# A reciprocal square root seeded by a power on GpSimd, with one Newton step

## The chip, the core and the metric

One core of a Trainium2 chip runs the whole program. The metric is the device time of one execution in microseconds (us); the median of three runs is given. The engines of the core work in parallel, each through its own queue in a fixed order, and wait for each other at semaphores: TensorE (PE) multiplies matrices, VectorE (DVE) and ScalarE (ACT) do elementwise work, GpSimd (POOL) issues small DMAs and fills buffers here, and SyncE (SP) issues the DMAs of the weights.

## What is computed

Two blocks of a diffusion transformer, one after the other, on 256 tokens of width 1024, in float32. Each block has two layers, each layer a mixing and a feed-forward part, and each part is modulated by vectors that come from a conditioning input. The norms between and inside the parts are where a reciprocal square root is taken:

```python
def layer_norm(x, g, b):
    mu = jnp.mean(x, axis=-1, keepdims=True)
    var = jnp.mean(jnp.square(x - mu), axis=-1, keepdims=True)
    return (x - mu) * lax.rsqrt(var + 1e-5) * g + b

def rms_norm(x, g):
    return x * lax.rsqrt(jnp.mean(jnp.square(x), axis=-1, keepdims=True) + 1e-6) * g

# first block
x = layer_norm(x, ln0_g, ln0_b)
for layer in range(2):
    y = hybrid_mixer(x * (1 + scale) + shift, ...)   # scan, latent attention, spatial gating
    x = layer_norm(DN_ALPHA * x + (1 + gate) * y, ...)
    y = swiglu(...) if layer == 0 else moe_swiglu(...)   # 8 experts, top 2
    x = layer_norm(DN_ALPHA * x + (1 + gate) * y, ...)
# second block
for l in range(2):
    h = rms_norm(x, norm_mix) * (1 + sc_a) + sh_a
    ...   # two kinds of attention, with rms_norm of q, k and of each head's output
    x = x + g_a * (concat([o_m, o_d]) @ w_out)
    h = rms_norm(x, norm_ffn) * (1 + sc_f) + sh_f
    x = x + g_f * ((silu(h @ w_gate) * (h @ w_up)) @ w_down)
```

## The kernel before

The program runs eight steps: 1 and 3 are the hybrid mixers, 2 a dense feed-forward part, 4 the experts, 5 and 7 attention, 6 and 8 feed-forward parts. The 256 tokens are two tiles of 128 rows, t = 0 and 1, with tokens on partitions; the products want the transposed rows, so between the steps rows are normalised, then transposed on PE (L175), then scaled and shifted (make_h, L501 to L506, or make_hf, L483).

Every weight block is split into an exact high and low part, high by a cast on ACT (L147), low by a subtraction on DVE (L148), and multiplied three times (L166 to L168). These splits are most of DVE's and ACT's work. The modulation vectors are sums over rows of a big matrix, made on DVE (L292, L294, tile macc) and closed by PE (L171), in portions that are filled in behind other work.

The reciprocal square root is one helper, rsqrt(v, n), for n numbers on each of 128 partitions. It takes half of v (L182), a first guess by integer arithmetic on v's bit pattern (L184), and three Newton steps, each two instructions for n = 1 (L188, L193) and three for more (L190, L191, L193): 8 or 11 DVE instructions, each needing the one before. It is called 38 times: 14 times with n = 1 (twice in layer_norm at the start; in resid at the boundaries 1 to 2, 2 to 3, 3 to 4, 5 to 6, 6 to 7, 7 to 8, once for each token tile), twice with n = 2 in resid_rms between steps 4 and 5, and 22 times in the mixers and the attentions, with n from 2 to 16. What takes its result at a boundary is L562 or L564 for t = 0 on DVE, and for t = 1 L557 and L558, or L560, of which L558 and L560 are on ACT (at 2 to 3 both tiles take L562). In step 3 the norm of the latent attention is taken by L865 and L866, in step 5 the norm of queries and keys by L1377.

A scheduler sets the order of each engine's queue when the program is built; work that is filled in (splits, modulation) is kept behind the last instruction of the last normalisation by the method behind. In step 4 the gate's modulation sum (eight blocks of rows, L294, closed by L171 on PE) is put in before make_hf and the router, and PE's queue holds its L171 ahead of the transposes for the router.

Of the kernel before, what the change touches and what calls it, by code (L numbers as in the profile page):

```python
# [20 lines left out]
KD = 8  # L21
# [38 lines left out]
# the second block's attention, in units of four heads: Q queries and keys, V values, A attention, F modulation  # L60
# [3 lines left out]
class _Net:  # L64
# [22 lines left out]
    def phase(self, **sizes):  # L87
        """Scratch pools of one part of the program."""
# [34 lines left out]
    def behind(self):  # L123
        """Vector work that is issued behind the last normalisation's short steps."""
# [14 lines left out]
    def split_now(self, v):  # L139
        """Exact high and low parts of a [128, k, n] block: two lists of k tiles."""  # L140
# [18 lines left out]
    def mm3(self, out, a, b, start, stop):  # L159
        """out += a^T b, a and b given as exact (high, low) parts."""  # L160
# [17 lines left out]
    def rsqrt(self, v, n):  # L178
        """1/sqrt of v (> 0) to float32 accuracy."""
        V = self.nc.vector  # L180
        vh = self.sc([128, n])
        V.tensor_scalar(vh, v, 0.5, None, ALU.mult)  # L182
        y = self.sc([128, n])
        V.tensor_scalar(y.bitcast(I32), v.bitcast(I32), -0.5, float(0x5F3759DF - 2 ** 31), ALU.mult, ALU.add)  # L184
        for _ in range(3):
            u = self.sc([128, n])
            if n == 1:
                V.scalar_tensor_tensor(u, y, vh[:, 0:1], y, ALU.mult, ALU.mult)  # L188
            else:
                V.tensor_tensor(u, y, y, ALU.mult)  # L190
                V.tensor_tensor(u, u, vh, ALU.mult)  # L191
            y2 = self.sc([128, n])
            self.last = V.scalar_tensor_tensor(y2, u, 1.5, y, ALU.subtract, ALU.mult)  # L193
            y = y2
        return y

    def evac_split(self, ps, hi, lo, A=None, B=None):
        """ps [128, 2, n] in PSUM -> exact parts of ps * A + B (columns per middle index)."""
# [30 lines left out]
    def fill(self, n):  # L229
        """n more blocks of two rows of 128 of the modulation's product, behind the rest."""  # L230
# [220 lines left out]
    def two_rows(self, g, b):  # L451
# [3 lines left out]
        return gb  # L455

    def affine(self, x, g, b):
        """x * g + b in place, with rows g and b from DRAM."""
        V = self.nc.vector
        gb = self.two_rows(g, b)  # L460
        for t in range(2):
# [1141 lines left out]
```

## Time and profile before

| what | value |
|---|---|
| median of three runs | 2099.36 us (2097.38 to 2099.42) |
| the profiled execution's own span | 2100.0 us |
| PE busy | 1959.5 us, 93% of the span |
| DVE busy | 1658.0 us, 79%, 2512 instructions |
| ACT busy | 1208.3 us, 58% |
| POOL busy | 50.1 us, 2%, 98 instructions |

The page gives for each engine its busy time and its share of the span. Its fourth part follows the work that ended last back to the start, and tells for each engine what share of the span lies on that chain. The table by stretches tells the busy time of each engine in a piece of the span; what PE lacks to the length of the piece is time in which it stood still. A timeline's row is the start, the duration, the engine, the line of the program, the operation, and what it writes and reads; in brackets stands how long the engine had been idle and what ended that.

### The profile page before, as it was taken

What the parts mean: (1) busy time and instruction counts of PE and PEld (TensorE: products, weight loads), DVE (VectorE), ACT (ScalarE), POOL (GpSimd) and SP (SyncE); (2) the same over time, 40 slices, a digit from 0 to 9 for tenths busy, and PEclk for the clock granted to TensorE, in tenths of its full rate; (3) what the DMA queues carried; (4) which work ended last, traced back from release to release, by engine and by line L of the source; (5) the groups of instructions that cost most, each with busy time, mean ns of one, the idle gap of its engine ahead of it and who ended that gap; (6) DMA issues with size and microseconds to landing.
All of it is one profiled execution on the core that took longest, in us unless ns stands there. A gap on an engine that the chain in (4) does not pass through costs nothing.

```text
span 2100.0 us, 30041 instructions
## 1 busy us (share of the span) xinstructions
PE 1959.5 (93%) x11481; PEld 1681.4 (80%) x11481; DVE 1658.0 (79%) x2512; ACT 1208.3 (58%) x1817; POOL 50.1 (2%) x98
## 2 busy tenths in 40 slices
PE   3998999898599999999999999969989999998999
PEld 3887999886478787878778887858869998978998
DVE  6888977897588888888888888889778877667554
ACT  3454444452378767767776777755454446545442
POOL 4000000100000000000000000000000000000000
PEclk9999999998599999999999999979999999999999
DMA  9585998565489999899989999958339894326662
GB/s 319 181 287 202 339 331 308 177 224 204 141 300 360 328 339 334 317 358 346 340 322 348 344 360 351 360 181 278 124 132 346 322 320 147 121 87 214 203 199 80
DMA packets 283238, 555.25 MB, mean 264 GB/s; under 512 B 10172, under 2 KB 137520, under 8 KB 283088
## 3 DMA queue, kind: packets, MB, share of 16 engines
q1 hardware_dynamic: 280000, 549.49, 74.6%
q0 software_dynamic: 2656, 3.20, 0.8%
q8 instruction: 91, 1.49, 0.3%
q10 hardware_dynamic: 432, 0.58, 0.1%
q14 instruction: 59, 0.48, 0.1%
HBM read 552.19 MB, written 1.05 MB: 263 GB/s over the span
## 4 chain that ended last, share of the span: by engine, by line
PE 64%; DVE 5%; ACT 2%; issue 1%; DMA 1%; ACTq 0%; DVEq 0%
PE pp L167 12%; PE pp L168 11%; PE pp L166 11%; PE pa L634 6%; PE ya L167 4%; PE ya L166 4%; PE ya L168 4%; PE pp L175 3%; PE pj L166 1%; PE pj L167 1%; PE pj L168 1%; PE pp L171 1%; DVE lo L148 1%; PE sa L171 1%; ACT hi L147 1%
## 5 line engine op out<-in xcount | busy, mean ns | idle before, releaser
L148 DVE TENSOR_TENSOR lo<-raw,hi 128x1024 fp32r<-128x1024 f32 x660 | 787.5, 1220 | 193.1 <-ACT hi L147 191.5
L147 ACT CAST hi<-raw 128x1024 fp32r<-128x1024 f32 x660 | 668.4, 1051 | 393.6 <-PE pp L167 157.9
L166 PE MATMUL pp<-h,hi 128*128 128x256 f32 x960 | 274.4, 286 | 0.0
L168 PE MATMUL pp<-h,lo 128*128 128x256 f32 x960 | 271.6, 283 | 0.0
L167 PE MATMUL pp<-h,hi 128*128 128x256 f32 x960 | 271.5, 283 | 0.0
L148 DVE TENSOR_TENSOR lo<-rawx,hi 128x1024 fp32r<-128x1024 f32 x176 | 208.5, 1220 | 42.4 <-ACT hi L147 42.3
L294 DVE SCALAR_TENSOR_TENSOR macc<-raw,const,macc 128x1024 f32<-128x1024 f32 x168 | 215.3, 1281 | 6.6 <-DMA raw<-in_ada_w_dram 2.3
L167 PEld LDWEIGHTS pp<-h,hi 128*128 128x128 f32 x960 | 184.1, 192 | 1.9 <-issue 1.2
L166 PEld LDWEIGHTS pp<-h,hi 128*128 128x128 f32 x960 | 184.0, 192 | 1.8 <-ACT hi L147 1.0
L168 PEld LDWEIGHTS pp<-h,lo 128*128 128x128 f32 x960 | 184.1, 192 | 0.0
L147 ACT CAST hi<-rawx 128x1024 fp32r<-128x1024 f32 x176 | 176.5, 1048 | 11.9 <-PE pp L168 9.9
L166 PE MATMUL pj<-hi,h 128*128 128x256 f32 x576 | 169.6, 295 | 8.2 <-ACT h L505 3.7
L167 PE MATMUL pp<-lo,h 128*128 128x512 f32 (+1 forms) x480 | 174.6, 364 | 1.2 <-DVE lo L148 1.0
L166 PE MATMUL pp<-hi,h 128*128 128x512 f32 (+1 forms) x480 | 173.0, 361 | 0.0
L167 PE MATMUL pj<-lo,h 128*128 128x256 f32 x576 | 166.0, 290 | 0.8 <-DVE lo L148 0.8
L168 PE MATMUL pj<-hi,h 128*128 128x256 f32 x576 | 165.9, 290 | 0.0
L634 PE MATMUL pa<-hi,s 128*128 128x512 f32 x528 | 151.5, 396 | 0.0
L167 PE MATMUL pp<-lo,xe 128*128 128x512 f32 (+1 forms) x384 | 146.5, 382 | 1.3 <-DVE lo L148 1.0
L166 PE MATMUL pp<-hi,xe 128*128 128x512 f32 (+1 forms) x384 | 145.2, 379 | 0.0
L168 PE MATMUL pp<-hi,xe 128*128 128x512 f32 (+1 forms) x384 | 144.7, 377 | 0.0
L168 PE MATMUL pp<-hi,x 128*128 128x512 f32 (+1 forms) x384 | 143.2, 373 | 0.0
L167 PE MATMUL ya<-lo,s 128*128 128x512 f32 x352 | 141.9, 403 | 0.0
(481 smaller groups left out, 3563.3 us busy)
## 6 DMA issues: line engine op xcount, KB each, us to landing
raw<-in_moe_w_dram SPq DMA_DIRECT2D x176, 1024.0 KB, 6.1
rawx<-in_moe_w_dram SPq DMA_DIRECT2D x88, 1024.0 KB, 6.5
raw<-in_ada_w_dram SPq DMA_DIRECT2D x48, 1024.0 KB, 6.9
raw<-in_w_mod_dram SPq DMA_DIRECT2D x48, 1024.0 KB, 6.3
raw<-in_w_in_dram SPq DMA_DIRECT2D x42, 1024.0 KB, 5.8
raw<-in_ffn_w_dram SPq DMA_DIRECT2D x33, 1024.0 KB, 6.1
raw<-in_w_gate_dram SPq DMA_DIRECT2D x22, 1024.0 KB, 5.4
raw<-in_w_up_dram SPq DMA_DIRECT2D x22, 1024.0 KB, 5.5
```

Of the source, the lines that this page charges most:

```text
L147: self.nc.scalar.copy(h, v[:, z:z + m])
L148: self.nc.vector.tensor_tensor(l, v[:, z:z + m], h.bitcast(F32), ALU.subtract)
L166: mm(out, lhsT=a[0], rhs=b[0], start=start, stop=False)
L167: mm(out, lhsT=a[0], rhs=b[1], start=False, stop=False)
L168: mm(out, lhsT=a[1], rhs=b[0], start=False, stop=stop)
L171: self.nc.tensor.matmul(out, lhsT=lhsT, rhs=rhs, start=start, stop=stop)
L175: self.nc.tensor.transpose(out, in_, self.ident[:p, :p])
L294: V.scalar_tensor_tensor(acc, v[:, i], c, acc, ALU.mult, ALU.add)
L634: mm(accs[t][h], lhsT=y[ia][:, s], rhs=W[ib][:, h * 512:(h + 1) * 512], start=start and ia == 0 and ib == 0, stop=stop and ia == 1)
```

## The change

rsqrt takes its first guess as the power v^(-1/2) on GpSimd, against a constant tile mhalf that holds -0.5 (a new memset on POOL at the start), and runs one Newton step in place of three. DVE then runs three instructions for n = 1 (L184, L187, L192 of the changed file) and four for more (L184, L189, L190, L192), and POOL one (L182). The sign of half of v is turned, so that the step adds 1.5 where it subtracted. Comments and docstrings that are left out as well move the line numbers: what was L292 and L294 is L290 and L292, what was L327 is L325.

```diff
     def rsqrt(self, v, n):
         V = self.nc.vector
+        y = self.sc([128, n])
+        self.nc.gpsimd.tensor_tensor(y, v, self.mhalf[:, 0:1].to_broadcast([128, n]) if n > 1 else self.mhalf, ALU.pow)
         vh = self.sc([128, n])
-        V.tensor_scalar(vh, v, 0.5, None, ALU.mult)
-        y = self.sc([128, n])
-        V.tensor_scalar(y.bitcast(I32), v.bitcast(I32), -0.5, float(0x5F3759DF - 2 ** 31), ALU.mult, ALU.add)
-        for _ in range(3):
-            u = self.sc([128, n])
-            if n == 1:
-                V.scalar_tensor_tensor(u, y, vh[:, 0:1], y, ALU.mult, ALU.mult)
-            else:
-                V.tensor_tensor(u, y, y, ALU.mult)
-                V.tensor_tensor(u, u, vh, ALU.mult)
-            y2 = self.sc([128, n])
-            self.last = V.scalar_tensor_tensor(y2, u, 1.5, y, ALU.subtract, ALU.mult)
-            y = y2
-        return y
+        V.tensor_scalar(vh, v, -0.5, None, ALU.mult)
+        u = self.sc([128, n])
+        if n == 1:
+            V.scalar_tensor_tensor(u, y, vh[:, 0:1], y, ALU.mult, ALU.mult)
+        else:
+            V.tensor_tensor(u, y, y, ALU.mult)
+            V.tensor_tensor(u, u, vh, ALU.mult)
+        y2 = self.sc([128, n])
+        self.last = V.scalar_tensor_tensor(y2, u, 1.5, y, ALU.add, ALU.mult)
+        return y2
...
+        self.mhalf = self.tl("const", [128, 1], tag="mhalf")
+        nc.gpsimd.memset(self.mhalf, -0.5)
```

The scheduler orders the queues anew. The first place is the start of the program. POOL's queue there, before, from the end of the small operands' DMAs (b_mod is the bias of the second block's modulation):

```order
L391 DMA sh_126<-in_diff_subln_dram 2x128
L370 DMA sh_144<-in_b_mod_dram 96x128
L425 DMA t_391<-in_ssd_dt_bias_dram 128x8
L425 DMA t_393<-in_ssd_a_log_dram 128x8
L425 DMA t_395<-in_ssd_d_dram 128x8
```

And after; ISA is an entry that loads code for POOL, and L182 are the powers of the two token tiles:

```order
L391 DMA sh_128<-in_diff_subln_dram 2x128
L370 DMA sh_146<-in_b_mod_dram 96x128
L182 ISA
L182 TENSOR_TENSOR t_161<-t_155,const_105 128x1
L182 TENSOR_TENSOR t_180<-t_174,const_105 128x1
L425 DMA t_377<-in_ssd_dt_bias_dram 128x8
```

Both powers now stand behind the DMA issues of the small operands. DVE's queue at the start, after (macc_190 is the first modulation sum, macc_218 the second, t_155 is v of the first tile, L325 takes the first sum from PE):

```order
L445 TENSOR_SCALAR t_155<-t_154 128x1
L290 TENSOR_SCALAR macc_190<-raw_191,const_113 128x1024
...
L292 SCALAR_TENSOR_TENSOR macc_190<-raw_203,const_113,macc_190 128x1024 x2
L187 SCALAR_TENSOR_TENSOR t_165<-t_161,t_163 128x1
L192 SCALAR_TENSOR_TENSOR t_167<-t_165,t_161 128x1
L325 SCALAR_TENSOR_TENSOR col_207<-pp_208,const_119 128x8
L447 TENSOR_TENSOR t_156<-t_153,t_167 128x1
L290 TENSOR_SCALAR macc_218<-raw_219,const_113 128x1024
```

Before, all eight instructions of the first call and L447 stood ahead of the first sum; now the whole first sum stands ahead of the call's last two instructions.

The second place is the latent attention's norm in step 3, on DVE, before (t_4660 is v, dc and cb belong to the scan, L865 takes the result):

```order
L182 TENSOR_SCALAR t_4667<-t_4660 128x4
L184 TENSOR_SCALAR t_4669<-t_4660 128x4
L294 SCALAR_TENSOR_TENSOR macc_4652<-raw_4986,const_111,macc_4652 128x1024
L839 TENSOR_TENSOR dc_4567<-dc_4567,cb_4546 128x512
L190 TENSOR_TENSOR t_4671<-t_4669 128x4
L148 TENSOR_TENSOR lo_5237<-raw_5230,hi_5236 128x1024
L191 TENSOR_TENSOR t_4671<-t_4671,t_4667 128x4
L148 TENSOR_TENSOR lo_5267<-raw_5264,hi_5266 128x1024
L193 SCALAR_TENSOR_TENSOR t_4674<-t_4671,t_4669 128x4
...
L193 SCALAR_TENSOR_TENSOR t_4684<-t_4681,t_4679 128x4
...
L865 TENSOR_SCALAR g_4165<-g_4165,t_4684 128x256
```

And after:

```order
L184 TENSOR_SCALAR t_4593<-t_4584 128x4
L189 TENSOR_TENSOR t_4595<-t_4591 128x4
L292 SCALAR_TENSOR_TENSOR macc_4576<-raw_4900,const_113,macc_4576 128x1024
L839 TENSOR_TENSOR dc_4491<-dc_4491,cb_4470 128x512
L190 TENSOR_TENSOR t_4595<-t_4595,t_4593 128x4
L148 TENSOR_TENSOR lo_5131<-raw_5124,hi_5130 128x1024
L192 SCALAR_TENSOR_TENSOR t_4598<-t_4595,t_4591 128x4
L900 TENSOR_TENSOR t_4645<-kvl_4152,const_103 128x32
L901 TENSOR_TENSOR t_4646<-kvl_4152,const_103 128x32
L865 TENSOR_SCALAR g_4089<-g_4089,t_4598 128x256
```

L865 moved ahead of two of the splits (L148), two products of the scan (L839) and one L843 that stood between the Newton steps.

The third place is the boundary from step 3 to step 4 on DVE, the second token tile, before (macc_5523 is the sum of the gate, L557 the tile's normalisation, L1088 a split of the normalised rows for the experts):

```order
L549 TENSOR_SCALAR t_5405<-t_5406 128x1
...
L193 SCALAR_TENSOR_TENSOR t_5423<-t_5421,t_5419 128x1
L294 SCALAR_TENSOR_TENSOR macc_5523<-raw_5538,const_111,macc_5523 128x1024
L557 SCALAR_TENSOR_TENSOR t_5425<-t_5406,t_5423 128x1
L148 TENSOR_TENSOR lo_5672<-raw_5661,hi_5671 128x1024
L294 SCALAR_TENSOR_TENSOR macc_5523<-raw_5538,const_111,macc_5523 128x1024
L148 TENSOR_TENSOR lo_5676<-raw_5661,hi_5675 128x1024
L1088 TENSOR_TENSOR h_5625<-x_5367,x_5624 128x2048
```

And after:

```order
L549 TENSOR_SCALAR t_5291<-t_5292 128x1
...
L557 SCALAR_TENSOR_TENSOR t_5303<-t_5292,t_5301 128x1
L292 SCALAR_TENSOR_TENSOR macc_5401<-raw_5404,const_113,macc_5401 128x1024 x2
L292 SCALAR_TENSOR_TENSOR macc_5401<-raw_5408,const_113,macc_5401 128x1024
L1088 TENSOR_TENSOR h_5503<-x_5261,x_5502 128x2048
...
L148 TENSOR_TENSOR lo_5558<-raw_5541,hi_5557 128x1024
L292 SCALAR_TENSOR_TENSOR macc_5401<-raw_5416,const_113,macc_5401 128x1024
L148 TENSOR_TENSOR lo_5562<-raw_5541,hi_5561 128x1024
```

L557 stood behind seven of the gate's eight sums and stands ahead of all of them now; L1088 and three L148 stand ahead of the last of these sums, where one L148 did. PE's queue keeps its order there: the gate's L171, then the router's transposes.

## Rows read from the trace of the kernel before

**Rows 1.** Stretches: start:end, length, each engine's busy us (instructions), PE clock, DMA share.

```profile
517.00:566.00 49.00, 25.34 (x121) 20.48 (x120) 34.58 (x76) 12.05 (x15) 1.48 (x2) 0.63 0.56 194
566.00:1383.00 817.00, 804.59 (x3771) 651.41 (x3771) 688.12 (x674) 594.08 (x693) 2.68 (x5) 0.99 0.94 334
1410.00:1544.00 134.00, 128.57 (x910) 111.92 (x910) 104.17 (x287) 69.52 (x143) 1.46 (x2) 1.00 0.54 181
1763.00:1891.00 128.00, 125.97 (x887) 110.05 (x887) 93.20 (x290) 71.17 (x148) 0.00 (x0) 0.99 0.40 129
1891.00:1903.00 12.00, 5.70 (x28) 4.58 (x28) 11.48 (x34) 8.67 (x20) 0.00 (x0) 0.80 0.07 29
```

**Rows 2.** Page, fourth part: engines' shares of the chain that ended last.

```profile
PE 64%; DVE 5%; ACT 2%; issue 1%; DMA 1%; ACTq 0%; DVEq 0%
```

**Rows 3.** Newton instructions: duration ns min/median/max, first and last start.

```profile
L188 DVE SCALAR_TENSOR_TENSOR t<-t,t x42: 209/219/221, 9.5 to 1898.9; 128x1 f32<-128x1 f32 x42
L193 DVE SCALAR_TENSOR_TENSOR t<-t,t x114: 148/161/179, 9.8 to 1899.2; 128x1 f32<-128x1 f32 x42, 128x4 f32<-128x4 f32 x24, 128x16 f32<-128x16 f32 x24, 128x2 f32<-128x2 f32 x12
```

**Rows 4.** DVE timeline, 7 to 8: a one-column call, before and behind it.

```profile
1894.50 0.69 DVE L538 TENSOR_TENSOR x<-x,x 128x512 f32<-128x512 f32 x1
...
1895.10 0.15 DVE L182 TENSOR_SCALAR t<-t 128x1 f32<-128x1 f32 x1
...
1896.69 0.76 DVE L564 TENSOR_SCALAR x<-x,t 128x1024 f32<-128x1024 f32 x1
```

**Rows 5.** DVE timeline, 4 to 5: a two-column call, before and behind it.

```profile
1392.44 1.28 DVE L586 SCALAR_TENSOR_TENSOR x<-x,t,raw 128x1024 f32<-128x1024 f32 x1
1393.64 0.16 DVE L182 TENSOR_SCALAR t<-t 128x2 f32<-128x2 f32 x1
...
1395.66 2.48 DVE L589 SCALAR_TENSOR_TENSOR x<-x,t,raw 128x1024 f32<-128x1024 f32 x2
```

**Rows 6.** POOL timeline (four rows) and ACT's, of fills, issues, a hop, a load.

```profile
0.24 0.10 POOL L1590 MEMSET const-float32-0.0<- 128x1 f32 x1 [0.24 <-issue]
...
18.27 0.54 POOL L370 DMA_DIRECT2D sh<-in_b_mod_dram  x1
...
254.00 0.95 POOL L283 MEMSET macc<- 128x1024 f32 x1 [61.82 <-DVE lo L148]
255.24 0.52 POOL L284 DMA_DIRECT2D macc<-in_ada_b_dram  x1 [0.29 <-POOL macc L283]
...
2.06 1.28 ACT L359 ACT_TABLE_LOAD   x1 [2.06 <-issue]
```

**Rows 7.** DVE and PE timelines, start: between the two modulation sums, and after.

```profile
26.15 0.17 DVE L327 SCALAR_TENSOR_TENSOR col<-pp,const 128x8 f32<-128x8 f32 x1 [3.73 <-PE pp L171]
...
36.28 1.86 PE L171 MATMUL pp<-const,macc 128*128 128x1 f32 x8 [10.16 <-DVE macc L294]
```

**Rows 8.** DVE and PE timelines, step 3: the latent attention's norm, a later gap.

```profile
445.27 0.16 DVE L182 TENSOR_SCALAR t<-t 128x4 f32<-128x4 f32 x1
...
455.23 0.34 DVE L865 TENSOR_SCALAR g<-g,t 128x256 f32<-128x256 f32 x1
...
475.17 0.87 PE L175 MATMUL pa<-const,P 128*128 128x128 f32 x3 [4.01 <-DVE P L925]
```

**Rows 9.** DVE and PE timelines, step 4: the gate's sum and the transposes.

```profile
538.76 1.28 DVE L294 SCALAR_TENSOR_TENSOR macc<-raw,const,macc 128x1024 f32<-128x1024 f32 x1
...
541.39 2.29 DVE L1088 TENSOR_TENSOR h<-x,x 128x2048 fp32r<-128x2048 f32 x1 [0.21 <-ACT x L1087]
543.60 2.35 DVE L148 TENSOR_TENSOR lo<-raw,hi 128x1024 fp32r<-128x1024 f32 x2
...
540.14 3.48 PE L171 MATMUL pp<-macc,const 128*128 128x512 f32 x4 [13.88 <-DVE macc L294]
543.79 0.66 PE L175 MATMUL pp<-const,x 128*128 128x128 f32 x4 [0.17 <-ACT gate L251]
```

**Rows 10.** PE timeline, step 5: the wait that L1377 ends.

```profile
1435.41 0.39 PE L166 MATMUL pj<-hi,h 128*128 128x256 f32 x1 [1.79 <-DVE qk L1377]
```

## The prediction

> **What bounds the kernel now.** I read the page first, for busy shares and the chain of work that ended last, then the table by stretches for PE, then timelines of the places where PE stands still. TensorE (PE) is busy 93% of the span and holds 64% of the chain; VectorE (DVE) holds 5% of it [rows 2]. That share is not spread evenly. In the experts of step 4 PE works 804.59 of 817 us, and in step 7 125.97 of 128 [rows 1]: a shorter vector step there finds nobody waiting for it. In the stretches between steps it is the other way round: 25.34 of 49 us before the experts, and 5.70 of 12 us between steps 7 and 8 [rows 1], because PE needs normalised rows that a short serial chain on DVE and ScalarE (ACT) makes. So the change is to be costed call by call, at the calls whose result PE waits for, and not by the sum of the instructions that it takes away.
>
> **What one call costs now.** The order lists 2577 DVE instructions before and 2336 after: 241 fewer, of some 0.16 us each [rows 3], about 39 us of DVE time, nearly all beside a busy PE. What counts is the serial time of a call. With one column it is from the start of L182 at 1895.10 to the start of L564 at 1896.69: 1.59 us [rows 4]. With two columns it is from 1393.64 to 1395.66: 2.02 us [rows 5].
>
> **What one call will cost.** DVE hands v to GpSimd (POOL), POOL takes the power, POOL hands y back, then DVE runs the last step: with one column 0.22 and 0.16 us, with gaps some 0.43; with more columns three instructions of 0.16 [rows 3], some 0.6 with gaps. Call the time from v to a usable y "q". No row of before shows a power, or DVE handing to POOL. From below: a POOL memset of one column, 0.10 us [rows 6], and hops of nothing: q = 0.1. From above: a memset of 1024 columns, 0.95 us, and the POOL hop over a semaphore, 0.29 us, twice [rows 6]: q = 1.5. A power of 1 to 16 columns is in size nearest to the small memset, and it computes rather than fills; I take 0.2 for it, and two hops of 0.29: **q = 0.8**. An isolated call is then 0.8 + 0.43 = 1.23 against 1.59 with one column (-0.36), and 0.8 + 0.6 = 1.4 against 2.02 with more (-0.6). New is a wait: L187 or L189 stands on DVE's queue until y is there, and whatever is queued behind it stands too; at the boundaries that is only the call's own consumer, elsewhere splits (L148) and modulation (L294, after: L292) that can spare 0.8 us.
>
> **Where it lands: the boundaries.** 1 to 2, 2 to 3, 5 to 6, 6 to 7 and 7 to 8 each hold two one-column calls, one behind the other, and PE waits for both results. 7 to 8 is the pattern: L538 of half a row runs 0.69 us from 1894.50 [rows 4] beside the new power, so the first call can gain up to 0.8 there, the second 0.36 at most. I take 0.6 a boundary: **-3.1** for five (-0.4 to -0.8 each).
>
> **4 to 5.** Two two-column calls. In the first, an L586 of 1.28 us from 1392.44 stands between v and L182 [rows 5]; POOL works beside it, and three short instructions remain: up to -1.3. The second is isolated: -0.6. **-1.5**, a little under their sum.
>
> **Step 3, the latent attention's norm.** Here the gain is not in the call's own length. Its eleven instructions lie among splits, modulation and the scan's products: L182 starts at 445.27, and the consumer L865 at 455.23 [rows 8], ten microseconds for two of work, since each short step waits its turn in DVE's queue. After, three steps remain with one L292, one L839 and one L148 between them (the order shows it): 445.27, plus 1.2, 0.6 and 1.2 for these and five short steps of 0.16, gives L865 at about 449, 6 us earlier. Behind it comes the serial attention, in which PE has a 4.01 us gap before 475.17 [rows 8] and smaller ones. Not all 6 us arrive, since the scan's own products fill PE meanwhile: 0 to -6, I take **-3.5**, inside that gap.
>
> **Attention, steps 5 and 7.** In the call of 16 columns whose L1377 ends the wait of 1.79 us before 1435.41 [rows 10], L190 stands behind a split; with the power on POOL the result is there before that split. The whole of step 5 has 134.00 - 128.57 = 5.4 us without PE work [rows 1], and three later calls are isolated. 0 to -5, I take **-2.5**. Step 7 has 2.0 us in all [rows 1]: **-1.3**.
>
> **Start.** Here the power stands in POOL's queue behind the DMA issues of the small operands; the last of these starts at 18.27 and takes 0.54 [rows 6]. The order shows an extra entry, "ISA", right before the first power, a loading of code for POOL. Its price has no row; the nearest is ACT's table load, 1.28 us [rows 6], and from below nothing. Before, the calls at the start needed nothing from POOL. After, the scheduler puts the first modulation sum ahead of L187, so that it starts about 1.5 us earlier, and its PE sums no longer wait for the transposes; the power lands near 18.8 + 1.3 + 0.8 = 20.9, before PE has made those sums. The second sum, which started behind L327 at 26.15 and ended with PE at 36.28 [rows 7], starts some 2.4 us earlier, and takes the second call's six short instructions in, 1.0 us: -1.4 at best. **-1.0**. Of the load itself the Trainium skill, page "GPSIMD Engine Reference", section 2.1 Instruction dispatch, says that the first call to a freshly loaded kernel pays about 6 us; no run here shows it; by that the power would land near 25.6, the term would be about +0.9, and the sum 1.9 us higher.
>
> **Step 4, the place that goes the other way.** Before, the second row tile's call was interleaved with the eight L294 of the gate's sum. PE's queue holds the sum's L171 ahead of the transposes that feed the router, so the end of the sum sets the router: last L294 from 538.76, L171 at 540.14 [rows 9], 13.88 us of PE gap. After, L557 comes early, which lets ACT finish its copies early, and the scheduler puts L1088 (2.29 us [rows 9]) and three L148 (1.2 each) ahead of the last L292, and takes seven short steps (0.9) out. 2.2 + 2 x 1.15 more than before, less 0.9, plus 0.8 for the wait on POOL: +4.4 on L171. What was put forward is saved later: before, the first L483 stood behind two L148 that ended at 543.60 + 2.35 = 545.95, and its transposes were there at 543.79 + 0.66 = 544.45 [rows 9], 1.4 to 1.5 us of waiting that goes. Net **+3.2** (+2.5 to +4.5), and the experts behind it are PE-bound, so it stays.
>
> **The sum.** -1.0 - 3.1 - 3.5 + 3.2 - 1.5 - 2.5 - 1.3 = -9.7. The profiled span is 2100.0, 0.6 over the median; 2100.0 - 9.7 - 0.6 = 2089.7: **2090**. About 14 calls stand free on the chain, so each microsecond of q is worth 14: q = 0.3 gives 2083, q = 1.5 gives 2099.5.
>
> **Rivals.**
> *A slow power.* At every boundary PE then waits for POOL instead of DVE, and from q = 1.5 the sum turns: 0.7 us over my value times 14 calls eats the 9.7. For it: nothing on POOL in this trace computes, and a power is no add. Against it: only 1 to 16 columns. At q = 2.2, 2090 + 1.4 x 14 = 2110, slower; between 1.2 and 1.7 it is 2095 to 2103, no change.
> *A long load at the start.* The first power is needed about when PE is done with the first sum; each microsecond of load beyond some 4 comes through whole. At 10 us the start is +5 and the time 2096.
> *POOL and DVE get in each other's way.* The gain at 7 to 8 and 4 to 5 counts on the power running beside L538 and L586. If one of them shuts the other out, the power begins when they end: 0.45 lost at four boundaries, 0.7 at 4 to 5, 1 us each at step 3 and the attentions: 2090 + 5 = 2095. The trace of before has no such pair. The Trainium skill, page "SBUF — State Buffer", section Who interferes with whom, says that a VectorE instruction with two SBUF inputs contends with a GpSimd instruction that reads SBUF, for the whole instruction; L538, L586, L148 and L294 are of that kind, and by it this rival would be the case; no run here shows it.
> *Nothing moves.* If in step 3 and the attentions other work comes last, -7.3 goes, and the boundaries' -3.1, -1.5 and -1.0 stand against +3.2: 2097.
>
> **How the numbers follow.** About 0.2%, 4.2 us, is what a measurement here can tell from no change: faster is below 2095, slower above 2103.5. Forecast (q 0.3 to 1.1, terms as summed, 2083 to 2095): 0.50, all faster. Way barred: 0.14, half faster, half the same. Slow power: 0.18, of which 0.13 slower and 0.05 the same. Long load: 0.06, 0.04 the same and 0.02 slower. Nothing moves: 0.12, with 0.02 slower, if step 4's term is at its upper end and the start's with it, and 0.10 the same. Faster 0.57, same 0.26, slower 0.17. From 2083 to 2104 the range leaves out some 0.05 below and 0.15 above.
>
> **What would show it.** Right: in the trace after, the power of one column is under 0.4 us and y is used within 0.9 us of v; L865 of step 3 near 449; between 7 and 8 L564 starts 0.4 to 0.8 earlier after its v; the gate's L171 in step 4 comes some 4 us later than the shift up to there. Wrong: q over 1.5; a POOL span that begins only when L538 or L586 ends; L187 at the start after 26 us; a step-4 router that is not late, or a latent attention that starts earlier with the same PE gaps behind it.

## The result

The changed kernel took 2129.98 us (2128.26 to 2135.3) beside 2099.14 of the kernel before in the same comparison: a ratio of 1.0153, with an interval of 1.0138 to 1.0168. It is 31 us slower, where 10 us faster was forecast. The page of the changed kernel, its span, its busy times and the chain that ended last:

```profile
span 2126.1 us, 29871 instructions
PE 1968.2 (93%) x11481; PEld 1685.3 (79%) x11481; DVE 1627.4 (77%) x2274; ACT 1211.5 (57%) x1817; POOL 108.0 (5%) x137
PE 62%; DVE 5%; issue 2%; ACT 2%; POOL 2%; ACTq 0%; DVEq 0%; POOLq 0%
PE pp L167 12%; PE pp L168 11%; PE pp L166 11%; PE pa L634 6%; PE ya L167 4%; PE ya L166 4%; PE ya L168 4%; PE pp L175 2%; POOL t L182 2%; PE pp L171 1%; DVE lo L148 1%; PE sa L171 1%; PE pj L168 1%; PE pj L166 1%; PE pj L167 1%
```

POOL, which was not on the chain of [rows 2], now holds 2% of it, nearly all in L182, the power. DVE has less to do (1627.4 us beside 1658.0) and PE is busy for no less time, and the span is 26 us longer (the profiled execution of the changed kernel was the fastest of its four, so this is less than the 31 us between the medians).

Where that is shows in the distances between fixed places: the first product of a step (L166), and the first instruction of a boundary on DVE that multiplies the step's result with its gate.

| stretch | before, us | after minus before, us |
|---|---|---|
| start, to the first product of step 1 | 45.10 | 0.0 |
| boundary 1 to 2 | 17.62 | -1.2 |
| boundary 2 to 3 | 13.28 | -1.5 |
| step 3 | 125.17 | -3.1 |
| boundary 3 to 4, to the experts' first product | 60.05 | +0.9 |
| boundary 4 to 5 | 23.37 | -1.5 |
| **step 5, attention** | **136.76** | **+18.5** |
| boundary 5 to 6 | 12.55 | -1.0 |
| boundary 6 to 7 | 11.21 | +0.6 |
| **step 7, attention** | **129.54** | **+15.7** |
| boundary 7 to 8 | 12.19 | -0.3 |

The steps that the table leaves out are between -1.5 (the experts) and +0.6 (step 8). Up to step 5 the changed kernel is 7.9 us ahead. It then loses 34 in the two attentions. Those two stretches by engine, before:

```profile
1407.10:1543.80 136.70, 131.27 (x922) 114.64 (x921) 106.89 (x289) 72.42 (x151) 1.46 (x2) 0.99 0.55 183
1760.50:1890.00 129.50, 127.06 (x892) 111.12 (x893) 94.78 (x292) 73.64 (x152) 0.00 (x0) 0.99 0.39 125
```

And after; the columns are start and end, length, busy us of PE, PE's weight loads, DVE, ACT and POOL (with instructions), the granted clock of PE as a share of the full 2.4 GHz, the share of DMA and GB/s:

```profile
1399.20:1554.40 155.20, 141.38 (x922) 122.89 (x921) 99.74 (x233) 73.25 (x151) 20.22 (x10) 0.91 0.47 161
1770.60:1915.90 145.30, 130.90 (x890) 113.55 (x889) 85.63 (x236) 74.14 (x153) 17.83 (x8) 0.96 0.34 112
```

Two things are to be seen. PE stands still for 13.8 and 14.4 us, where it stood for 5.4 and 2.4: 20.3 us more. And the same products cost PE 272.3 us where they cost 258.3: 14.0 more, at a granted clock of 0.91 and 0.96, where it was 0.99. Of the two levels that the clock has, 1.2 and 2.4 GHz, the lower one fills the second of these two stretches nearly whole, right behind one in which PE had work for 8.98 of 12 us:

```profile
1496.00:1508.00 12.00, 8.98 (x52) 8.39 (x51) 4.99 (x15) 3.03 (x5) 2.90 (x1) 0.72 0.27 87
1508.00:1520.00 12.00, 12.00 (x47) 8.41 (x47) 7.10 (x26) 4.74 (x17) 0.00 (x0) 0.56 0.28 89
```

What fills the gaps is the power. POOL's groups after, one row for each width; the mean of one in ns is the last number ahead of the second bar:

```profile
L182 POOL TENSOR_TENSOR t<-t,const 128x16 f32<-128x16 f32 x8 | 25.0, 3128 | 96.3 <-DVE t L1374 91.5 <-ACT y L204 4.8
L182 POOL TENSOR_TENSOR t<-t,const 128x1 f32<-128x1 f32 x14 | 10.6, 754 | 193.4 <-DVE t L552 92.9 <-DVE t L549 91.9 <-DVE t L445 8.4
L182 POOL TENSOR_TENSOR t<-t,const 128x4 f32<-128x4 f32 x8 | 10.0, 1250 | 107.7 <-DVE t L1454 78.2 <-DVE t L862 22.7 <-DVE t L992 6.8
L182 POOL TENSOR_TENSOR t<-t,const 128x8 f32<-128x8 f32 x4 | 7.5, 1872 | 63.9 <-DVE t L1452 63.9
L182 POOL TENSOR_TENSOR t<-t,const 128x2 f32<-128x2 f32 x4 | 4.0, 1008 | 300.8 <-DVE t L583 214.4 <-DVE t L954 81.9 <-DVE t L592 4.6
```

Undisturbed it takes 0.56 us for one column, 0.70 for two, 1.01 for four, 1.64 for eight and 2.90 for sixteen: 0.40 us and 0.157 for each column. The 16 calls inside the attentions are of 16, 8 and 4 columns. One of them in step 7, on DVE, POOL and PE (the start, the duration, in brackets the idle time and its end):

```profile
1807.72 0.17 DVE L1374 TENSOR_SCALAR t<-t 128x16 f32<-128x16 f32 x1
1807.93 0.18 DVE L184 TENSOR_SCALAR t<-t 128x16 f32<-128x16 f32 x1
...
1810.91 0.18 DVE L189 TENSOR_TENSOR t<-t 128x16 f32<-128x16 f32 x1 [2.81 <-POOL t L182]
...
1812.56 0.68 DVE L1377 TENSOR_TENSOR qk<-pj,t 128x512 f32<-128x512 f32 x1
...
1807.97 2.90 POOL L182 TENSOR_TENSOR t<-t,const 128x16 f32<-128x16 f32 x1 [17.20 <-DVE t L1374]
...
1814.57 0.66 PE L175 MATMUL pp<-const,qk 128*128 128x128 f32 x4 [3.75 <-DVE qk L1392]
```

v is there at 1807.89, and y is used at 1810.91: q = 3.02 us. DVE stands for 2.81 us behind L189, and PE for 3.75 until the rotated keys come. The list of waits has, in step 5 and in step 7 (the total, how often, the longest):

```profile
DVE t L189 <- POOL t L182: 14.6, 7, 2.9
...
DVE t L189 <- POOL t L182: 15.8, 8, 2.8
```

### The profile page after: what moved, and what is told of

Its sections match the earlier page's. It is cut to its first block, busy times and chain, and to the rows that moved or that the text cites. A ratio compares the mean times of both kernels' runs of the same rounds, so it can differ in the third digit from the quotient of the medians.

```text
span 2126.1 us, 29871 instructions
## 1 busy us (share of the span) xinstructions
PE 1968.2 (93%) x11481; PEld 1685.3 (79%) x11481; DVE 1627.4 (77%) x2274; ACT 1211.5 (57%) x1817; POOL 108.0 (5%) x137
## 3 DMA queue, kind: packets, MB, share of 16 engines
q8 instruction: 91, 1.49, 0.3%
HBM read 552.19 MB, written 1.05 MB: 260 GB/s over the span
## 4 chain that ended last, share of the span: by engine, by line
PE 62%; DVE 5%; issue 2%; ACT 2%; POOL 2%; ACTq 0%; DVEq 0%; POOLq 0%
PE pp L167 12%; PE pp L168 11%; PE pp L166 11%; PE pa L634 6%; PE ya L167 4%; PE ya L166 4%; PE ya L168 4%; PE pp L175 2%; POOL t L182 2%; PE pp L171 1%; DVE lo L148 1%; PE sa L171 1%; PE pj L168 1%; PE pj L166 1%; PE pj L167 1%
## 5 line engine op out<-in xcount | busy, mean ns | idle before, releaser
L148 DVE TENSOR_TENSOR lo<-raw,hi 128x1024 fp32r<-128x1024 f32 x660 | 787.4, 1221 | 206.6 <-ACT hi L147 205.2
L166 PE MATMUL pp<-h,hi 128*128 128x256 f32 x960 | 274.4, 286 | 0.0
L148 DVE TENSOR_TENSOR lo<-rawx,hi 128x1024 fp32r<-128x1024 f32 x176 | 208.5, 1220 | 40.9 <-ACT hi L147 40.9
L292 DVE SCALAR_TENSOR_TENSOR macc<-raw,const,macc 128x1024 f32<-128x1024 f32 x168 | 215.3, 1282 | 9.9 <-DMA raw<-in_ada_w_dram 3.9
L166 PEld LDWEIGHTS pp<-h,hi 128*128 128x128 f32 x960 | 184.0, 192 | 1.8 <-ACT hi L147 1.2
L166 PE MATMUL pj<-hi,h 128*128 128x256 f32 x576 | 171.0, 298 | 5.8 <-DVE qk L1377 3.5
L166 PE MATMUL pp<-hi,h 128*128 128x512 f32 (+1 forms) x480 | 173.0, 361 | 0.3 <-ACT h L505 0.3
L168 PE MATMUL pj<-hi,h 128*128 128x256 f32 x576 | 168.8, 295 | 0.4 <-DVE h L506 0.4
L166 PE MATMUL pp<-hi,xe 128*128 128x512 f32 (+1 forms) x384 | 144.6, 377 | 0.0
```

The source lines that it names most:

```text
L148: self.nc.vector.tensor_tensor(l, v[:, z:z + m], h.bitcast(F32), ALU.subtract)
L166: mm(out, lhsT=a[0], rhs=b[0], start=start, stop=False)
L168: mm(out, lhsT=a[1], rhs=b[0], start=False, stop=stop)
L292: V.scalar_tensor_tensor(acc, v[:, i], c, acc, ALU.mult, ALU.add)
```

## The experiments

### The attentions' calls taken back

```diff
     def rsqrt(self, v, n):
+        if self.step in (5, 7) and n > 1:
+            return self.rsqrt_bits(v, n)   # as before: bit-pattern seed, three steps
```

> The 16 calls inside the two attentions (4 to 16 columns) go back to the bit-pattern seed and three Newton steps; the other 22 keep the power on GpSimd. From the trace of the changed kernel the other calls had gained 7.9 us by the start of step 5, some 1 at each of the two later boundaries, and the two attentions lost 18 and 16. Theory (the loss is in the attentions alone): 2099.1 - 9 = 2090, 2087 to 2093. Rival (a loss that is spread, such as a slower start or a power that costs something at every call): over 2099.

Measured: 2096.64 us beside 2100.56 of before, ratio 0.9979 (0.9970 to 0.9989). The loss is gone, and with it any other place for it: steps 5 and 7 are back to -0.4 and -1.1 against before. But the time is not 2090. The 9 us were read from one trace; in this one step 3 gained 1.9 and not 3.1, the boundary 3 to 4 lost 2.0 and not 0.9, steps 1, 2 and 8 lost 0.7, 0.6 and 1.8. Of a gain outside the attentions some 4 us are left, just over what can be told from none.

### Only the calls of 16 columns taken back

```diff
     def rsqrt(self, v, n):
+        if n == 16:
+            return self.rsqrt_bits(v, n)
```

> Only the 8 calls of 16 columns (queries and keys) go back to the bit-pattern seed; the 8 calls on the heads' outputs (8 and 4 columns) keep the power. Theory of length (the power takes 0.40 us plus 0.157 a column in the trace, so a call of 16 columns loses 1.6 us where it stands alone, one of 8 columns 0.3, and one of 4 gains 0.25): nearly all of the loss goes, 2091 to 2095. Rival of a fixed price (what costs is the hand-over between the engines, alike for all 16 calls): half of the 34 us goes, about 2113.

Measured: 2099.31 us, ratio 0.9994 (0.9985 to 1.0004). In the trace, steps 5 and 7 stand at +0.3 and +0.6 against before. So the eight calls of 16 columns make 33 of the 34 us, 4 us each, and the eight of 8 and 4 columns 1 to 2.4 in all (2.7 by the medians of this run and the one ahead of it); a fixed price for each call is out. The median is above the 2091 to 2095 that I expected. The execution that was traced took 2094.06 us, the fastest of the ten, so where the others lost some 5 us no trace shows.

### The same hand-over with a short operation

```diff
-        self.nc.gpsimd.tensor_tensor(y, v, self.mhalf[:, 0:1].to_broadcast([128, n]) ..., ALU.pow)
+        if self.step in (5, 7) and n > 1:
+            self.nc.gpsimd.tensor_tensor(y, v, v, ALU.subtract)
+        else:
+            self.nc.gpsimd.tensor_tensor(y, v, self.mhalf[:, 0:1].to_broadcast([128, n]) ..., ALU.pow)
```

> As the changed kernel, in the same order on every engine, but inside the attentions GpSimd subtracts v from itself in place of the power, so that the attentions' normalised values are zero; the hand-over from VectorE to GpSimd and back stays. Theory of length: the loss goes and the attentions gain, 2083 to 2091. Rival of the hand-over or of the new order of the queues: 2120 to 2130, as the changed kernel.

Measured: 2098.56 us, ratio 0.9993 (0.9983 to 1.0003). The order on DVE, PE and ACT is the changed kernel's, row by row. The two attentions in this kernel, and what POOL does there:

```profile
1402.50:1539.70 137.20, 135.07 (x922) 117.26 (x921) 99.45 (x234) 73.20 (x151) 4.94 (x10) 0.95 0.54 183
1756.20:1885.50 129.30, 126.95 (x890) 110.84 (x889) 85.18 (x235) 74.03 (x153) 2.58 (x8) 0.99 0.40 125
```
```profile
L183 POOL TENSOR_TENSOR t<-t 128x16 f32<-128x16 f32 x8 | 3.5, 436 | 98.7 <-DVE t L1377 98.7
```

With an operation of 0.44 us in the place of one of 3.13, the loss is gone: neither the hand-over nor the order made it. PE stands for 2.1 and 2.3 us, where it stood for 5.4 and 2.4 before. But the attentions do not gain: 137.2 and 129.3 us, as before's 136.7 and 129.5. Here PE's products took 3.7 us more (262.0) at a clock of 0.95 in step 5, which took back what the shorter waits gave. That fall of the clock came without a wait. PE had work for 11.44 of the 12 us ahead of it, and then ran mostly at the lower level for 10 us:

```profile
1481.00:1493.00 12.00, 11.44 (x98) 11.10 (x96) 9.73 (x25) 5.50 (x7) 0.42 (x2) 1.00 0.53 175
1493.00:1503.00 10.00, 10.00 (x34) 6.20 (x34) 5.11 (x20) 5.32 (x17) 0.00 (x0) 0.56 0.34 108
```

Why it fell is open. So of the 14.0 us by which the changed kernel's products are dearer, some 4 can come without its waits. The theory of length holds for the loss; the gain that my expectation added to it, 2083 to 2091, was wrong.

### The same powers with nobody waiting

```diff
+        if self.step in (5, 7) and n > 1:
+            d = self.sc([128, n])
+            self.nc.gpsimd.tensor_tensor(d, v, self.mhalf[:, 0:1].to_broadcast([128, n]), ALU.pow)
+            return self.rsqrt_bits(v, n)
```

> As the kernel with the bit-pattern seed in the attentions, and GpSimd takes the same 16 powers besides, for nobody: no instruction waits for them. Theory of length (what costs is VectorE's queue standing behind the instruction that waits for the power): the same time as without them, 2088 to 2093. Rival of the port (a running power shuts VectorE's two-input instructions out, or slows them): 2100 or more, with splits in the attentions that take well over 1.22 us.

Measured: 2097.09 us, ratio 0.9988 (0.9977 to 0.9998), as without these powers. The splits (L148) of the two attentions; the columns are the stretch, its length, DVE's busy us, the granted clock, the share of DMA and GB/s:

```profile
1403.60:1539.10 135.50, 33.25 (x28) 0.99 0.55 185
1755.20:1884.20 129.00, 34.58 (x29) 0.99 0.39 126
```

That is 1.19 us a split, as in the kernel without these powers (67.95 us for the same 57). So some 37 us of POOL's work beside DVE's cost nothing; it is the waiting that costs.

### The power twice

```diff
+        if self.step in (5, 7) and n > 1:
+            self.nc.gpsimd.tensor_tensor(y, v, self.mhalf[:, 0:1].to_broadcast([128, n]), ALU.pow)
         self.nc.gpsimd.tensor_tensor(y, v, ..., ALU.pow)
```

> As the changed kernel, but inside the two attentions GpSimd takes each power twice, the second over the first, so that each call waits for both. The added length is the sum of these 16 powers, about 36 us. Theory (the length of the power comes through one to one, since PE waits for the call and VectorE's queue stands): 2130 + 30 to 36 = 2160 to 2166. Rival (most of the 30 us comes from the new order, or from the first of the two hops): 2130 to 2142.

Measured: 2176.48 us, ratio 1.0360 (1.0338 to 1.0382): 46 us over the changed kernel, more than one to one. The two attentions:

```profile
1402.00:1576.00 174.00, 145.29 (x919) 127.11 (x919) 99.66 (x233) 73.50 (x151) 37.07 (x18) 0.88 0.43 144
1793.00:1963.00 170.00, 139.65 (x885) 121.17 (x886) 85.42 (x235) 74.41 (x153) 33.79 (x16) 0.88 0.29 94
```

Of the 43.5 us that these two stretches are longer than after's, PE stands for 30.8 more (59.1 beside 28.2) and works 12.7 longer on the same products, at a clock of 0.88. Put in a row: some 6 us of short operations in the attentions give 266.5 us, 36.6 us of powers 300.5, some 70 us 344. Each microsecond of POOL's time costs 1.1 to 1.3: some 0.8 to 0.9 as PE's waiting, and 0.3 to 0.4 because the same products take longer at a lower granted clock. This is an average over calls with very different prices: of the 30.6 us between the first two kernels of this row 21.5 lie in the calls of 16 columns, which make 33 of the 34 us, and 9 in the others, which make 1 to 2.4.

### The gate's sum in step 4

```diff
-        if self.step in (5, 7) and n > 1:
+        if self.step in (5, 7) and n > 1 or self.step == 3 and n == 1:
             return self.rsqrt_bits(v, n)
```

> As the kernel with the bit-pattern seed in the attentions, and the two calls at the boundary from step 3 to step 4 go back to it too, so that the gate's modulation sum is again ahead of L1088 and the splits. Theory of the order (there the change lets the gate's sum end later, which PE's queue holds ahead of the router): the stretch from the boundary's first instruction to the first expert product, 62.0 us in that kernel and 60.1 before, goes back to 60 to 60.5, and the time falls by 0.5 to 2 us, to about 2095.5. Rival (the shorter call pays for the later sum): the stretch stays, or grows by up to 1.

Measured: 2094.47 us, ratio 0.9968 (0.9955 to 0.9980). Against the kernel that it is cut from (0.9970 to 0.9989) the total tells nothing, since the intervals overlap. The place does: from the second tile's statistics to the gate's L171 it was 12.28 us before and 17.6 to 17.9 in each of the six kernels that have the new order there, and it is 12.28 again here; to the router's second round of products it was 30.0, then 31.2 to 33.2, and is 30.1. The stretch I had named went from 62.0 to 61.4, not to 60: the second tile's statistics came 12.7 us behind the boundary's first instruction, where it was 11.6 before, and why is open.

### Two steps on VectorE, without GpSimd

```diff
-        V.tensor_scalar(y.bitcast(I32), v.bitcast(I32), -0.5, float(0x5F3759DF - 2 ** 31), ALU.mult, ALU.add)
-        for _ in range(3):
+        V.tensor_scalar(y.bitcast(I32), v.bitcast(I32), -0.5, float(0x5F376908), ALU.mult, ALU.add)
+        for k in (1.50087896, 1.50000057):
...
-            self.last = V.scalar_tensor_tensor(y2, u, 1.5, y, ALU.subtract, ALU.mult)
+            self.last = V.scalar_tensor_tensor(y2, u, k, y, ALU.subtract, ALU.mult)
```

> The kernel before, with VectorE alone: the bit-pattern seed with another constant and two Newton steps with slightly changed constants in place of three, in all 38 calls (largest relative error about 7e-7). A call of one column has 6 instructions and is 0.45 us shorter, one of more has 8 and is 0.6 shorter, without a hop and without GpSimd. Theory (only the length of the isolated calls counts): as much as the power gains at the boundaries and the attentions' isolated calls besides, 2092 to 2096. Rival (the gain outside the attentions needs VectorE's work to go to another engine): 2097 to 2101.

Measured: 2095.68 us, ratio 0.9975 (0.9963 to 0.9986). The seven boundaries gave 0.5 to 1.8 us each, 6.3 in all: shorter isolated calls are what gains, and they need no other engine. In the attentions this kernel is at -0.2 and -0.1 too: three instructions less in each of 16 calls, and nothing comes of it.

### Put together

```diff
+        if n > 1 and self.step != 4 or n == 1 and self.step == 3:
+            return self.rsqrt_bits(v, n)   # two steps, as in the run ahead of this one
```

> A kernel put together from what the runs showed: the power on GpSimd only for the calls of one or two columns that PE waits for at the boundaries (and at the start), without the boundary from step 3 to step 4; two Newton steps with changed constants on VectorE everywhere else. By the stretches of the earlier runs: the boundaries with the power give 1.25, 1.8, 1.5, 1.1 and 0.5 us, the boundary 3 to 4 with two steps 1.5, the start 0.7: 2100.3 - 7 = 2093, 2091 to 2095. Rival (gains at the boundaries are lost again in the PE-bound steps behind them): 2095 to 2098, as with either alone.

Measured: 2094.45 us, ratio 0.9974 (0.9964 to 0.9985), inside the expected 2091 to 2095 but against a kernel before of 2098.86. By the ratio it is no better than its parts, and the rival of 2095 to 2098 is not ruled out. The boundaries give what they gave (-1.4, -1.8, -1.5, -1.2, -0.5), steps 1, 2 and 8 and the boundary 6 to 7 take 2.2 back, and the boundary 3 to 4, from which 1.5 was expected, stands at +0.2.

### The power and VectorE side by side

```python
z = max(src[:, 0:n], y)                      # VectorE, n columns, after the last power
scalar_tensor_tensor(two, w, z[:, 0:1], x)   # VectorE, 1024 columns; or one input, or one from PSUM
y = pow(z, mhalf)                            # GpSimd
```

> A small kernel that leaves the network out: VectorE and GpSimd alone, a chain of powers of 1 to 32 columns, then powers that begin together with one long VectorE instruction (two inputs from SBUF; one input from SBUF; one from PSUM and one from SBUF), then powers of 32 columns under which VectorE instructions begin. Theory of the shared port, read from the trace of the changed kernel (a power of two columns took 1.67 us beside an L586 and 0.70 alone): the power beside a two-input instruction is longer by what that instruction still has to run, 0.7 to 1.1 us, and 0.56 (1 column) and 2.9 us (16) beside the one with one input from SBUF and one from PSUM. Rival (the long powers are long for another reason, such as GpSimd waking up): no difference between the three kinds. For the way back, a two-input instruction that begins under a running power of 5.4 us: held until the power ends (port rule both ways), or not held (a power reads its few columns at its beginning).

Alone, powers of 1 to 16 columns took 0.56, 0.70, 1.01, 1.63 and 2.89 us here, and one of 32 took 5.41. From the end of DVE's z to the power's start it was 0.08 us, from the power's end to DVE's next instruction 0.03: **q is the power and 0.11 us**. A power that began together with a two-input instruction was not held (0.56 and 2.91 us); the instruction took 1.31 and 1.34 us. Beside a tensor_scalar that began with it, the power of one column took 0.77, 0.21 more than alone, and the one of 16 columns 2.91, no more. Nor were two-input instructions held that began under a running power of 5.41 us: three took 2.08 us, as three from PSUM did (2.07). So I had the start of it wrong, and a second kernel put the power's begin under a VectorE instruction that was already running:

```diff
-y = pow(z, mhalf)                            # begins together with the VectorE instruction
+y1 = pow(z[:, 0:1], mhalf)
+y2 = pow(y1 over m columns, mhalf)           # begins when the VectorE instruction is under way
```

> A small kernel that leaves the network out. GpSimd takes a power of one column and then, from its result, one of 1 or 16 columns, which so begins some 0.85 us after VectorE has begun two long instructions: none (control), two inputs from SBUF (1.3 us each), one input from SBUF (0.7 each), one from PSUM and one from SBUF (0.75 each). In the pairs that began together a power was not held. Theory (a two-input instruction that has already begun keeps GpSimd's reads out until it ends): the second power is 0.4 to 0.5 us longer beside two inputs from SBUF, 0.56 and 2.9 in the control and beside PSUM. Rival (the long powers in the changed kernel have another cause): no difference between the four.

The second powers, in the order none, two inputs from SBUF, one from SBUF, one from PSUM and one from SBUF, each with 1 and with 16 columns; ahead of the third stand the two VectorE instructions beside it:

```profile
8.89 0.56 POOL L119 TENSOR_TENSOR y<-y,mhalf 128x1 f32<-128x1 f32 x1
10.62 2.91 POOL L119 TENSOR_TENSOR y<-y,mhalf 128x16 f32<-128x16 f32 x1
...
14.02 2.50 DVE L87 SCALAR_TENSOR_TENSOR two<-w,z,x 128x1024 f32<-128x1024 f32 x2
14.69 1.05 POOL L119 TENSOR_TENSOR y<-y,mhalf 128x1 f32<-128x1 f32 x1
17.50 3.40 POOL L119 TENSOR_TENSOR y<-y,mhalf 128x16 f32<-128x16 f32 x1
...
22.29 0.95 POOL L119 TENSOR_TENSOR y<-y,mhalf 128x1 f32<-128x1 f32 x1
24.62 3.31 POOL L119 TENSOR_TENSOR y<-y,mhalf 128x16 f32<-128x16 f32 x1
...
29.10 0.55 POOL L119 TENSOR_TENSOR y<-y,mhalf 128x1 f32<-128x1 f32 x1
30.82 2.91 POOL L119 TENSOR_TENSOR y<-y,mhalf 128x16 f32<-128x16 f32 x1
```

Beside two inputs from SBUF the power is 0.49 us longer (1.05 and 3.40). The first instruction had begun 14.69 - 14.02 = 0.67 us earlier and ran to 15.33; the power of one column ended at 15.74, 0.41 behind it, so most of its work came after. Beside one from PSUM and one from SBUF it is not longer. Beside the instruction with one input from SBUF (a tensor_scalar of float32) it is 0.4 longer, too. The Trainium skill, page "SBUF — State Buffer", section Who interferes with whom, says both, the second for tensor_scalar in its two-port modes, and that whoever issues first gets the ports; that part agrees. By the same rule a DVE instruction that begins under a running power would wait, and it did not (2.08 us for three, above); the power's few columns seem to be read at its begin, which no run here shows by itself.

## Why the prediction was wrong, step by step

**The step that failed** is "A power of 1 to 16 columns is in size nearest to the small memset ...; I take 0.2 for it, and two hops of 0.29: q = 0.8". One value for all widths was wrong, and so was the upper end of 1.5, which was a fill of 1024 columns and two hops. For one column it came out nearly right, by two errors that cancel: 0.56 for the power and 0.11 for both hops, q = 0.67. For 16 columns q is 3.0. A call of 16 then takes 3.0 + 0.6 = 3.6 where one of 2 columns took 2.02 [rows 5]. The rows of before had the widths of the calls, and I never asked what a column costs.

**The second step that failed** is the place. The rival of a slow power was priced by "About 14 calls stand free on the chain", that is, by the boundaries, where calls have one or two columns. It was the attentions, which I had entered with -2.5 and -1.3. Even with a short operation they give nothing (+0.4 and -0.2 with the subtraction, -0.2 and -0.1 with two steps). With the subtraction PE stood for 3.4 us less in the two attentions, and its products took 3.7 more. A gap that opens instead cost more than itself in the changed kernel: 20.3 us of standing came with 14.0 of dearer products.

**The wait that the change adds** was named and priced at nothing: "splits (L148) and modulation (L294, after: L292) that can spare 0.8 us". In the call shown above DVE has only L184 ahead of L189, nothing that could fill 2.8 us; DVE stood for 30.4 us in the two attentions, as the rows of its waits show.

**The boundaries, -3.1:** measured -1.2, -1.5, -1.0, +0.6 and -0.3, in all -3.5. In the other runs 1 to 2, 2 to 3, 5 to 6 and 7 to 8 came out at -1.2 to -1.4, -1.6 to -1.8, -1.0 to -1.2 and -0.3 to -0.5. At 6 to 7 there is no gain in any run with the power, and the order on ACT is why: PE's first product there waits for ACT's L505, which in each of these kernels stands behind the second tile's L560 now (L560 from 1768.92, L505 to 1770.59, L166 at 1770.64). Before, and in the kernel with two steps on VectorE, which gained 0.9 there, L505 stands ahead of L560. 7 to 8 after, as in [rows 4]:

```profile
1920.24 0.15 DVE L552 TENSOR_SCALAR t<-t 128x1 f32<-128x1 f32 x1
1920.30 0.68 DVE L538 TENSOR_TENSOR x<-x,x 128x512 f32<-128x512 f32 x1
...
1921.43 0.22 DVE L187 SCALAR_TENSOR_TENSOR t<-t,t 128x1 f32<-128x1 f32 x1 [0.39 <-POOL t L182]
...
1921.88 0.75 DVE L564 TENSOR_SCALAR x<-x,t 128x1024 f32<-128x1024 f32 x1
...
1920.46 0.93 POOL L182 TENSOR_TENSOR t<-t,const 128x1 f32<-128x1 f32 x1 [16.15 <-DVE t L552]
1923.02 0.56 POOL L182 TENSOR_TENSOR t<-t,const 128x1 f32<-128x1 f32 x1 [1.63 <-DVE t L552]
```

From v at 1920.39 to L564 it is 1.49 us; before it was 1.59 from L182 on, and L538 was ahead of that, so the call gained 0.6. The power beside L538 took 0.93, 0.37 over its 0.56. The second one, alone, took 0.56.

**4 to 5, -1.5:** measured -1.5 in each run with the power. The first call shows the rival of the barred way, and the second the undisturbed one:

```profile
1386.04 1.28 DVE L586 SCALAR_TENSOR_TENSOR x<-x,t,raw 128x1024 f32<-128x1024 f32 x1
...
1386.22 1.67 POOL L182 TENSOR_TENSOR t<-t,const 128x2 f32<-128x2 f32 x1 [214.39 <-DVE t L583]
1392.46 0.70 POOL L182 TENSOR_TENSOR t<-t,const 128x2 f32<-128x2 f32 x1 [4.57 <-DVE t L592]
```

The power of two columns ends at 1387.89, 0.57 behind the end of L586 at 1387.32. So this rival was right as a mechanism, and the gain of 1.5 us came all the same. All 38 powers together took 57.1 us where undisturbed they would take 48.5; in the attentions they are 2.7 us longer by it, which cannot make 34.

**Step 3, -3.5, is a third step that failed,** though the number looks right. L865 came at 446.65, 8.6 earlier than in [rows 8]; 3.0 of that is v, which came earlier, and 5.4 us from v to L865 where it was 11.0 is 5.6 in the call, where 6 was forecast. But PE's waits did not shrink by it. The whole stretch, before and after:

```profile
391.12:516.29 125.17, 115.57 (x741) 101.86 (x742) 110.23 (x224) 61.12 (x134) 2.37 (x7) 0.90 0.65 219
388.44:510.55 122.11, 111.91 (x741) 98.72 (x742) 108.75 (x202) 61.24 (x134) 8.53 (x16) 0.94 0.68 232
```

PE stood for 9.6 us before and for 10.2 after; the 3.1 us are the same 741 products at a granted clock of 0.94 where it was 0.90. In the other kernels with the power there it is alike: the stretch gained 1.9 to 2.6 in the four with a clock of 0.94, and 0.0 and 0.8 in the two with 0.91 and 0.90, and PE stood for 9.8 us or more in each. So the gain came by luck, and the prediction had named this sign of being wrong itself (a latent attention that starts earlier with the same PE gaps behind it). Whether the change raised the clock there is not shown.

**Step 4, +3.2:** the order did what it was read to do. L1088 and the gate's L171 after, to set beside [rows 9]:

```profile
527.02 2.28 DVE L1088 TENSOR_TENSOR h<-x,x 128x2048 fp32r<-128x2048 f32 x1
...
539.12 3.51 PE L171 MATMUL pp<-macc,const 128*128 128x512 f32 x4 [16.69 <-issue]
```

From the second tile's statistics L1088 is 8.1 us earlier, and L171 5.3 later (4.4 was forecast); in the six kernels with this order 1.2 to 3.2 of that reach the router. With the first tile's shorter call in it the stretch is at +0.9 here, and at +0.2 to +2.0 in the others.

**Start, -1.0:** measured 0.0, and -0.7 to +0.3 in the other runs. POOL's queue had the first power where the order had it; the power, DVE's L187 and the sums on PE:

```profile
L182 POOLq MODIFY_POOL_CONFIG  x2: 37/37/37, 18.9 to 18.9; - x2
...
19.00 1.56 POOL L182 TENSOR_TENSOR t<-t,const 128x1 f32<-128x1 f32 x1
29.00 1.53 POOL L182 TENSOR_TENSOR t<-t,const 128x1 f32<-128x1 f32 x1 [8.45 <-DVE t L445]
...
21.37 0.21 DVE L187 SCALAR_TENSOR_TENSOR t<-t,t 128x1 f32<-128x1 f32 x1
```

The order's ISA entry is MODIFY_POOL_CONFIG here: 37 ns, and the power begins 0.1 behind it. The first power takes 1.56 us, with an L292 beside it that runs from 18.85 to 20.13; it ends 0.43 behind that, as the held power of the small kernel did (0.41). So the code load adds nothing that these rows show; the 6 us that the Trainium skill gives on its page "GPSIMD Engine Reference", section 2.1 Instruction dispatch, appear neither here nor in the small kernels, whose first power took 0.56. The rival of the long load falls with it. What the first sum gained by its earlier place it lost again: the second call's instructions now stand inside the second sum, and PE's L171 of that sum came at 36.39 (36.28 in [rows 7]).

The sum without the attentions was forecast at -5.9. The changed kernel was 7.9 ahead at step 5 (3.1 of it by the clock in step 3), and the kernel with the attentions taken back is 3.9 ahead in all. The boundaries and 4 to 5 were right in size; the start gave nothing, step 3 gave nothing by its mechanism, and step 4 cost less than forecast. The working has small slips that decide nothing: the traces have 238 DVE instructions fewer, not 241; five boundaries at 0.6 are 3.0, not 3.1; step 4's 4.4 less 1.4 to 1.5 is 2.9 to 3.0, not 3.2; and the items of the barred way add to 5.5, not 5.

## What to carry to other kernels

Before an operation is moved to another engine, its time there has to be known for the sizes that the calls have, the widest above all; where no row shows it, a small kernel with that operation at each width gives it before the change is built, and an upper end that is taken from another operation is not an upper end. A wait that is put into an in-order queue costs what the queue has nothing to fill, and where TensorE waits for it, its granted clock can fall and make the same products dearer: here 34 us, of which 20 were waiting and 14 a slower clock (some 4 of these can come without a wait). A stretch that got shorter is no proof of the mechanism that was priced for it: what the engine stood still and what its work took have to be read apart. Where many short serial steps are to be cut, cutting steps on the engine that has them (two in place of three) gave as much as the hand-over.

## What the runs showed of the hardware

- A power on GpSimd, float32 on 128 partitions, took 0.40 us and 0.157 for each column (0.56 at 1, 2.90 at 16, 5.41 at 32).
- The hand-over from VectorE to GpSimd took 0.08 us and the way back 0.03, where 0.29 had been read from a hop inside GpSimd's own queue that ended in a DMA issue.
- A power that begins under a running VectorE instruction with two inputs from SBUF does most of its work behind that one's end (0.49 us longer in the small kernel, 0.97 beside L586); beside a float32 tensor_scalar of 1024 columns from SBUF it took 0.40 longer, beside one input from PSUM and one from SBUF it is not held, and a running power did not hold VectorE (three instructions in 2.08 us under it).
- PE's time for the same products in the attentions was 258.3, 272.3 and 284.9 us, with 7.9, 28.2 and 59.1 us of standing still among them; with 4.5 us of standing still it was 262.0, since the clock fell once behind a stretch in which PE had work for 11.44 of 12 us.
